# Two pairs of idle transpositions in each gated projection of a decoder trunk, and two other moves on TensorE

## The chip, the cores and the metric

One NeuronCore of a Trainium2 chip. The metric is the time of one execution in device microseconds (us); less is better. Several executions of the same program are given with their median.

## What is computed

Two layers. In each, a gated feed-forward block (SwiGLU, half step), a token mixer of 16 heads in three groups, and a second gated block; at the end a norm. The batch is 1, there are T = 256 tokens, D = 1024 channels, and FF = 2816 hidden channels. All data are float32.

```python
def _rmsnorm(x, g):
    x32 = x.astype(jnp.float32)
    y = x32 * lax.rsqrt(jnp.mean(x32 * x32, axis=-1, keepdims=True) + RMS_EPS)
    return (y * g.astype(jnp.float32)).astype(x.dtype)

def _swiglu(x, w_gate, w_up, w_down):
    return (jax.nn.silu(x @ w_gate) * (x @ w_up)) @ w_down
...
    for l in range(DEPTH):
        x = x + 0.5 * _swiglu(_rmsnorm(x, ffn1_norm[l]), ffn1_w_gate[l], ffn1_w_up[l], ffn1_w_down[l])
        h = _rmsnorm(x, mix_norm[l])
...
        x = x + jnp.concatenate([out_a, out_b, out_c], axis=-1) @ w_out[l]
        x = x + 0.5 * _swiglu(_rmsnorm(x, ffn2_norm[l]), ffn2_w_gate[l], ffn2_w_up[l], ffn2_w_down[l])
    return _rmsnorm(x, final_norm)
```

The heads of the mixer add a bias that depends on the distance of query and key alone, out of a table of 32 rows by 16 heads (`rel_bias_table`).

## The kernel before

**Layout and precision.** x lies transposed in SBUF, channels on partitions: `xs` is 8 blocks of 128 channels by 256 tokens. Weights come as float32 in chunks of 128 x 1024, two chunks to a load of 1 MB on SP's DMA queue, into five buffers (`raw`, RAW = 5). `split` (lines 144 to 160) makes of each chunk a rounded part `whi` (ACT, line 157) and the rest `wlo` (DVE, line 158), three chunks ahead of their use. The operands of x are split likewise into `xx[k]`, both parts side by side. A product of 128 channels by 128 outputs is then two matmuls (`mm2`, lines 289 to 292): `whi` against both parts, 512 columns, and `wlo` against the first, 256 columns. This text calls the two a pair.

**Order on TensorE (PE).** Matmuls and transpositions are chained in the order in which the code issues them (`in_order`, line 211), so nothing overtakes on PE. All other engines' instructions and the DMAs are ordered by the framework's scheduler.

**A gated projection** (`ffn`, line 307; four in all, called first, second, third and fourth here) has 22 steps i of two chunks, 16 pairs each: gate and up sums of 128 hidden channels in two PSUM banks (`pgu`). 352 pairs in all. Then 8 x 22 = 176 pairs of the down projection follow (`pdn`). The norm isn't applied to x ahead of the products: its factor is worked out while they run, and multiplies the sums afterwards. For that, `norm.column()` (matmuls `pss` of the squares' sum against ones, then `ms` on DVE and `rcol` on POOL) is issued behind the first pair of step 2, and `rms_row` (two transpositions `prow` and a copy `rrow` on DVE) behind the tenth pair of it. Counted from 0 over the projection, these pairs are tiles 32 and 41. The constant `AT = (0, 9)` counts them within step 2.

**PSUM** has four banks with the tag "mm" and four with "at". The sums of steps 2, 5, 8 ... lie in "at", as do `pss`, `prow`, the bias table's products and most of the mixer's small results. A tile of a tag waits until an earlier one of the tag has been read.

**The bias table.** `load_bias` (line 387) issues four small loads on SP's queue and comes at step 3 of the first projection; `make_bias` (line 399) comes at step 6: two products `pu` of the table against one-hot distances, a copy each to SBUF on DVE, and a chain of DMAs on SP's queue: rows `u` to memory, 128 copies of them (`w`), and back as `bias` in the form that the mixer adds.

**The end.** The last projection's down products give a block k of x every 22 pairs. DVE adds it to x (lines 366 and 295), ACT squares two blocks at a time (line 243), POOL adds the squares up, ACT makes `y` (x by the gain, line 371, tag "A" with three buffers), and PE transposes it into `turned` (`turn`, line 375): block k - 1 behind the down products of block k, so inside the stream. Behind the last block come `pss` on the earlier sum and on both last squares, turn 7, `ms`, `rcol`, the scaling of `turned` and the store.

Of the kernel before, what the change touches and what calls it, by code (L numbers as in the profile page):

```python
# [39 lines left out]
AT = (0, 9)  # L40
# [38 lines left out]
def tile_trunk(ctx, tc, xT, gains, kvg, sinks, table, onehot, wgu, wdn, winv, wins, wkv, wout, out):  # L79
# [146 lines left out]
    class Norm:  # L226
# [11 lines left out]
        def square(self, k, last=False, after=None):  # L238

            if k % 2 == 0:  # L240
                return
            sq = tmp.tile([P, 2, T], F32, tag="sq2", name="sq", bufs=2)
            behind(nc.scalar.activation(sq, xs[:, k - 1:k + 1, :], AF.Square), after)  # L243
            if len(self.sums) == 0 or (last and k == DK - 1):
                self.sums.append(sq)
            else:
                s = tmp.tile([P, 2, T], F32, tag="ss", name="ss", bufs=2)
                nc.gpsimd.tensor_add(s, self.sums[0], sq)  # L248
                self.sums = [s]
            if k == DK - (3 if last else 1):  # L250
                s = tmp.tile([P, T], F32, tag="fold", name="fold", bufs=1)
                nc.gpsimd.tensor_add(s, self.sums[0][:, 0, :], self.sums[0][:, 1, :])
                self.sums = [s]
            elif k == DK - 1:
                self.sums = [self.sums[0], sq[:, 0, :], sq[:, 1, :]]
# [51 lines left out]
    def ffn(norm, nxt, last=False, first=None, between=(), at=AT):  # L307
        hs, banks, ws = [], {}, {}

        def products(i, h, start=0, stop=DK):  # L310

            if start == 0:
                ws[0] = next_w(ahead=(i, h) not in ((1, 1), (2, 0)))
                if h == 0:
                    for m in range(2):
                        banks[i, m] = bank("pgu", "at" if i % 3 == 2 else "mm")
            whi, wlo = ws[0]
            for j in range(start, stop):
                k, m = h * DK // 2 + j // 2, j % 2
                c = slice(j * P, (j + 1) * P)  # L320
                mm2(banks[i, m], whi[:, c], wlo[:, c], xx[k], k == 0, k == DK - 1)


        products(0, 0)
        products(0, 1)
        if first:
            first()
        products(1, 0)
        products(1, 1)
        for n in range(2 * DK):  # L330
            products(2, n // DK, n % DK, n % DK + 1)
            if n == at[0]:
                col = norm.column()
                for m in range(2):
                    split(cursor[0] + SPLIT_AHEAD - 2 + m)
            if n == at[1]:
                row = rms_row(col)
        for i in range(FK):
# [7 lines left out]
            nc.vector.tensor_mul(t, g, row)  # L346
# [3 lines left out]
            nc.gpsimd.tensor_mul(sr, s, row)  # L350
# [5 lines left out]
        for k in range(DK):  # L356
# [7 lines left out]
            if last and k:  # L364
                turn(k - 1)
# [3 lines left out]
            if last:  # L369
                ys[k] = tmp.tile([P, T], F32, tag="A", name="y")  # L370
                nc.scalar.activation(ys[k], x[k], AF.Copy, scale=nxt.g(k))
# [15 lines left out]
    def load_bias():  # L387
        nc.sync.dma_start(out=kvgain, in_=kvg)
# [3 lines left out]
        tab = tmp.tile([NBUCK + 1, NH], F32, tag="tab", name="tab", bufs=1)  # L392
        nc.vector.memset(tab[NBUCK:NBUCK + 1, :], NEG)
        nc.sync.dma_start(out=tab[:NBUCK, :], in_=table)
        oh = act.tile([NBUCK + 1, 2, NDIST], F32, tag="oh", name="onehots")
        nc.sync.dma_start(out=oh, in_=onehot)
        early.extend((tab, oh))
# [331 lines left out]

    for l in range(DEPTH):  # L730
        nxt = Norm(3 * l + 1)
        ffn(norm, nxt, first=first_squares if l == 0 else None, between={3: load_bias, 6: make_bias} if l == 0 else {})
# [95 lines left out]
```

## Time and profile before

| what | us |
|---|---|
| median of three executions | 966.33 |
| these three | 972.0, 965.53, 966.33 |
| the profiled execution | 971.86 |
| its span, from the first instruction to the last | 970.1 |
| PE busy in it | 957.8 |
| DVE, ACT and POOL busy | 689.7, 554.5, 182.5 |

The profile comes from one more execution, whose own time stands in the table; the difference between its time and its span lies around the program. The records of matmuls have modelled ends, so distances between their starts tell more than their durations. A product of two float32 operands (`pu`, `pss`) leaves two records, a transposition one.

### The profile page before, as it was taken

Reading aid. Unit: us, or ns where it says so; the run is one execution under the profiler, and the core shown is the slowest. Engines: PE = TensorE matmul, PEld = TensorE weight load, DVE = VectorE, ACT = ScalarE, POOL = GpSimd, SP = SyncE. Lnnn points to the kernel's source line nnn. Section 1 sums busy time; section 2 is a strip of 40 time slices with the busy share of each in tenths; the row PEclk is TensorE's granted clock in tenths of the full one; section 3 lists DMA queues with packets and bytes.
Section 4 is the critical chain, followed back from the end, with each engine's and each line's share of the span. In section 5 each row is a group of like instructions: output and inputs, shape, how many; then the busy total and the mean of one; then the engine's idle time right before and its main releaser. Section 6 shows DMA issues by size and latency. Waiting matters only on the chain.

```text
span 970.1 us, 15601 instructions
## 1 busy us (share of the span) xinstructions
PE 957.8 (99%) x5924; PEld 846.5 (87%) x5924; DVE 689.7 (71%) x1235; ACT 554.5 (57%) x1024; POOL 182.5 (19%) x156
## 2 busy tenths in 40 slices
PE   8999999999999999999999999999999999999996
PEld 7888888898999888888888888889989988888885
DVE  5787775659747877776668777666795588777552
ACT  6655554446876655554446556544488566555442
POOL 3221110121313212210022211001132042211001
PEclk9999999999999999999999999999999999999998
DMA  8688545553424565555556555555433346555511
GB/s 336 222 301 296 201 174 179 178 188 126 156 93 174 178 212 175 177 198 189 175 179 208 177 190 201 175 181 190 150 130 133 131 174 217 174 180 202 184 44 43
DMA packets 47575, 174.41 MB, mean 180 GB/s; under 512 B 3291, under 2 KB 5867, under 8 KB 47372
## 3 DMA queue, kind: packets, MB, share of 16 engines
q1 hardware_dynamic: 47212, 172.90, 51.3%
q8 instruction: 46, 0.75, 0.3%
q10 hardware_dynamic: 288, 0.52, 0.1%
q14 instruction: 29, 0.24, 0.1%
HBM read 172.34 MB, written 4.22 MB: 182 GB/s over the span
## 4 chain that ended last, share of the span: by engine, by line
PE 90%; issue 3%; DVE 2%; ACT 2%; POOL 1%; DMA 1%; SPq 0%; POOLq 0%; DVEq 0%; ACTq 0%
PE pgu L215 50%; PE pdn L215 22%; PE pp L215 7%; PE pwo L215 5%; PE pv L215 2%; PE po L215 1%; PE pt L218 1%; POOL ss L248 1%; PE psc L215 1%; DVE acc L499 1%; ACT whi L157 1%; DMA raw<-wgu 1%; DVE m L498 1%; ACT e L576 0%; PE pi L215 0%
## 5 line engine op out<-in xcount | busy, mean ns | idle before, releaser
L215 PE MATMUL pgu<-xx,whi 128*128 128x512 f32 x1408 | 498.1, 398 | 1.6 <-ACT whi L157 1.6
L158 DVE TENSOR_TENSOR wlo<-raw,whi 128x1024 fp32r<-128x1024 f32 (+3 forms) x314 | 383.3, 1223 | 141.2 <-ACT whi L157 134.4
L157 ACT CAST whi<-raw 128x1024 fp32r<-128x1024 f32 (+2 forms) x322 | 332.6, 1034 | 250.0 <-PE pdn L215 110.4
L215 PE MATMUL pgu<-xx,wlo 128*128 128x256 f32 x1408 | 396.0, 281 | 0.0
L215 PEld LDWEIGHTS pgu<-xx,whi 128*128 128x128 f32 x1408 | 265.1, 188 | 66.0 <-ACT whi L157 1.9
L215 PEld LDWEIGHTS pgu<-xx,wlo 128*128 128x128 f32 x1408 | 266.8, 189 | 0.3 <-DVE wlo L158 0.3
L215 PE MATMUL pdn<-h,whi 128*128 128x512 f32 x704 | 248.5, 397 | 0.0
L215 PE MATMUL pdn<-h,wlo 128*128 128x256 f32 x704 | 197.6, 281 | 0.0
L350 POOL TENSOR_TENSOR sr<-s,rrow 128x256 f32<-128x256 f32 x88 | 98.0, 1113 | 357.4 <-ACT s L348 357.1
L215 PEld LDWEIGHTS pdn<-h,whi 128*128 128x128 f32 x704 | 132.1, 188 | 31.7
L215 PEld LDWEIGHTS pdn<-h,wlo 128*128 128x128 f32 x704 | 133.0, 189 | 0.0
L302 ACT COPY b<-pgu 128x256 f32<-128x256 f32 x176 | 65.3, 372 | 82.2 <-PE pgu L215 82.2
L304 DVE TENSOR_TENSOR a<-pgu,b 128x256 f32<-128x256 f32 x176 | 73.5, 420 | 26.1 <-ACT b L302 25.5
L215 PE MATMUL pp<-xx,whi 128*128 128x256 f32 x480 | 90.7, 289 | 0.0
L215 PEld LDWEIGHTS pp<-xx,whi 128*128 128x128 f32 x480 | 74.2, 191 | 2.7 <-issue 1.7
L215 PE MATMUL pp<-xx,wlo 128*128 128x256 f32 x240 | 67.7, 282 | 0.0
L352 DVE TENSOR_TENSOR h<-sr,a 128x256 f32<-128x256 f32 x88 | 37.4, 425 | 29.0 <-POOL sr L350 28.7
L215 PE MATMUL pwo<-ohl,whi 128*128 128x256 f32 x256 | 47.7, 287 | 0.0
L248 POOL TENSOR_TENSOR ss<-sq 128x512 f32<-128x512 f32 x7 | 10.2, 1457 | 196.8 <-ACT sq L243 196.8
L215 PEld LDWEIGHTS pp<-xx,wlo 128*128 128x128 f32 x240 | 45.8, 191 | 0.0
L354 ACT CAST h<-h 128x256 fp32r<-128x256 f32 x88 | 35.3, 401 | 18.3 <-DVE h L352 18.3
L348 ACT ACTIVATE s<-t 128x256 f32<-128x256 f32 x88 | 37.4, 425 | 5.8 <-DVE t L346 5.5
(99 smaller groups left out, 718.1 us busy)
## 6 DMA issues: line engine op xcount, KB each, us to landing
raw<-wgu SPq DMA_DIRECT2D x86, 1024.0 KB, 5.0
raw<-wdn SPq DMA_DIRECT2D x44, 1024.0 KB, 5.0
raw<-wins SPq DMA_DIRECT2D x14, 1024.0 KB, 4.9
raw<-wout SPq DMA_DIRECT2D x8, 1024.0 KB, 4.9
raw<-winv SPq DMA_DIRECT2D x4, 776.0 KB, 4.2
w<-u SPq DMA_DIRECT2D x1, 3072.0 KB, 13.9
bias<-w SPq DMA_DIRECT2D x1, 2048.0 KB, 9.9
raw<-wgu SPq DMA_DIRECT2D x3, 512.0 KB, 7.7
```

Source lines behind the costliest of these rows:

```text
L157: ops = (nc.scalar.copy(hi[:, a:b], raw(n, a, b)), low.tensor_sub(lo[:, a:b], raw(n, a, b), f(hi[:, a:b])))
L158: low.tensor_sub(lo[:, a:b], raw(n, a, b), f(hi[:, a:b])))
L215: in_order(nc.tensor.matmul(*a, **kw))
L218: in_order(nc.tensor.transpose(*a))
L248: nc.gpsimd.tensor_add(s, self.sums[0], sq)
L302: nc.scalar.copy(b, p[:, T:])
L304: nc.vector.tensor_add(a, p[:, :T], b)
L348: nc.scalar.activation(s, t, AF.Silu)
L350: nc.gpsimd.tensor_mul(sr, s, row)
L352: nc.vector.tensor_mul(h, sr, u)
L354: nc.scalar.copy(hs[i][:, 0, :], h)
L498: nc.vector.max(out=m8, in_=acc[:, cs])
```

## The change

It does six things.

1. `ffn` counts its pairs through (`tile_no`), and `AT = (32, 41)` names the same two places as before.
2. Behind tiles 44 and 48 of each of the four projections a bank of the tag "at", called `step`, is taken, and two transpositions of the identity are written to it. Nobody reads them.
3. `make_bias` is issued in the first projection behind tile 32, ahead of `norm.column()`, in place of step 6. The loads of the table and the one-hots go to ACT's DMA queue and are issued ahead of the first projection (`load_bias`); the mixer's small scales keep their place at step 3 (`load_scales`).
4. In the last projection, `turn(0)` to `turn(6)` are issued in one run behind the down products of block 7, no longer one by one between them.
5. `y` lies in the buffers of the tags "E" and "ET", four each, instead of "A".
6. For the last norm, the squares of blocks 6 and 7 are taken one by one; POOL adds the square of block 6 to the sum, so `pss` has two operands there, not three.

```diff
-AT = (0, 9)
+
+
+AT = (32, 41)
+STEP = (44, 48)
...
         def square(self, k, last=False, after=None):
 
+            if last and k > DK - 3:
+                sq = tmp.tile([P, T], F32, tag="sq2", name="sq", bufs=2)
+                nc.scalar.activation(sq, x[k], AF.Square)
+                if k == DK - 2:
+                    s = tmp.tile([P, T], F32, tag="ss", name="ss", bufs=2)
+                    nc.gpsimd.tensor_add(s, self.sums[0], sq)
+                    self.sums = [s]
+                else:
+                    self.sums.append(sq)
+                return
             if k % 2 == 0:
                 return
...
-            if len(self.sums) == 0 or (last and k == DK - 1):
+            if len(self.sums) == 0:
...
-            elif k == DK - 1:
-                self.sums = [self.sums[0], sq[:, 0, :], sq[:, 1, :]]
...
-    def ffn(norm, nxt, last=False, first=None, between=(), at=AT):
+    def ffn(norm, nxt, last=False, first=None, ahead=None, between=()):
...
+        tile_no = [0]
+        col, row = [], []
+
+        def products(i, h):
+
+            whi, wlo = next_w(ahead=(i, h) not in ((1, 1), (2, 0)))
+            if h == 0:
+                for m in range(2):
+                    banks[i, m] = bank("pgu", "at" if i % 3 == 2 else "mm")
+            for j in range(DK):
                 k, m = h * DK // 2 + j // 2, j % 2
                 c = slice(j * P, (j + 1) * P)
                 mm2(banks[i, m], whi[:, c], wlo[:, c], xx[k], k == 0, k == DK - 1)
...
+                if tile_no[0] == AT[0]:
+                    if ahead:
+                        ahead()
+                    col.append(norm.column())
+                    for m in range(2):
+                        split(cursor[0] + SPLIT_AHEAD - 2 + m)
+                if tile_no[0] == AT[1]:
+                    row.append(rms_row(col[0]))
+                if tile_no[0] in STEP:
+                    p = bank("step", "at")
+                    for b in range(2):
+                        transpose(p[:, b * P:(b + 1) * P], ident, ident)
+                tile_no[0] += 1
+
+
+        for i in range(3):
+            for h in range(2):
+                products(i, h)
+            if i == 0 and first:
+                first()
...
-            if last and k:
-                turn(k - 1)
+            if last and k == DK - 1:
+                for i in range(k):
+                    turn(i)
...
             if last:
-                ys[k] = tmp.tile([P, T], F32, tag="A", name="y")
+                ys[k] = tmp.tile([P, T], F32, tag=("E", "ET")[k % 2], name="y", bufs=4)
                 nc.scalar.activation(ys[k], x[k], AF.Copy, scale=nxt.g(k))
...
     def load_bias():
+        tab = tmp.tile([NBUCK + 1, NH], F32, tag="tab", name="tab", bufs=1)
+        nc.vector.memset(tab[NBUCK:NBUCK + 1, :], NEG)
+        nc.scalar.dma_start(out=tab[:NBUCK, :], in_=table)
+        oh = act.tile([NBUCK + 1, 2, NDIST], F32, tag="oh", name="onehots")
+        nc.scalar.dma_start(out=oh, in_=onehot)
+        early.extend((tab, oh))
+
+    def load_scales():
         nc.sync.dma_start(out=kvgain, in_=kvg)
...
+    load_bias()
     for l in range(DEPTH):
         nxt = Norm(3 * l + 1)
-        ffn(norm, nxt, first=first_squares if l == 0 else None, between={3: load_bias, 6: make_bias} if l == 0 else {})
+        if l == 0:
+            ffn(norm, nxt, first=first_squares, ahead=make_bias, between={3: load_scales})
+        else:
+            ffn(norm, nxt)
```

On PE, behind the first pair of step 2 of the first projection, stood before (whi and wlo are the weight's parts, xx the operand of x, fold the sum of the squares):

```order
L215 MATMUL pgu<-xx_103,whi_184 128x512 [waits Activation_49]
L215 MATMUL pgu<-xx_103,wlo_185 128x256 [waits DVE_49]
L215 MATMUL pss<-ones,fold 128x1 [waits Pool_49]
L215 MATMUL pss<-ones,fold 128x1
L215 MATMUL pgu<-xx_103,whi_184 128x512
```

and stands now:

```order
L218 MATMUL pgu<-xx_103,whi_189 128x512 [waits Activation_49]
L218 MATMUL pgu<-xx_103,wlo_190 128x256 [waits DVE_49]
L218 MATMUL pu<-onehots,tab 8x384 [waits DMAHW2_49,DMAHW0_49]
L218 MATMUL pu<-onehots,tab 8x384
L218 MATMUL pss<-ones,fold 128x1 [waits PE_49,Pool_49]
L218 MATMUL pss<-ones,fold 128x1
L218 MATMUL pgu<-xx_103,whi_189 128x512 [waits DVE_49]
```

The two products of the bias table have come in ahead of pss, and the pair behind pss waits for DVE, which gives a bank back.

On PE, at the tenth pair of step 2 of the second projection, stood before (rcol is the norm's factor by token):

```order
L218 MATMUL prow<-ident,rcol 128x128 [waits Pool_49]
L218 MATMUL prow<-ident,rcol 128x128
L215 MATMUL pgu<-xx_108,whi_3509 128x512
L215 MATMUL pgu<-xx_108,wlo_3510 128x256
L215 MATMUL pgu<-xx_108,whi_3509 128x512
L215 MATMUL pgu<-xx_108,wlo_3510 128x256
L215 MATMUL pgu<-xx_109,whi_3509 128x512
L215 MATMUL pgu<-xx_109,wlo_3510 128x256
L215 MATMUL pgu<-xx_109,whi_3509 128x512
```

and stands now:

```order
L221 MATMUL prow<-ident,rcol 128x128 [waits Pool_49]
L221 MATMUL prow<-ident,rcol 128x128
L218 MATMUL pgu<-xx_108,whi_3515 128x512
L218 MATMUL pgu<-xx_108,wlo_3516 128x256
L218 MATMUL pgu<-xx_108,whi_3515 128x512
L218 MATMUL pgu<-xx_108,wlo_3516 128x256
L218 MATMUL pgu<-xx_109,whi_3515 128x512
L218 MATMUL pgu<-xx_109,wlo_3516 128x256
L221 MATMUL step<-ident 128x128 [waits DVE_49]
L221 MATMUL step<-ident 128x128
L218 MATMUL pgu<-xx_109,whi_3515 128x512
```

Three pairs behind prow the first step has come in; the second stands four pairs further.

On PE, at the program's end, stood before (pdn are the down products, y the blocks to be turned):

```order
L215 MATMUL pdn<-h_10041,wlo_10474 128x256
L218 MATMUL turned<-ident,y 128x128 [waits Activation_49]
L218 MATMUL turned<-ident,y 128x128
L215 MATMUL pss<-ones,fold 128x1 [waits Pool_49]
L215 MATMUL pss<-ones,fold 128x1
L215 MATMUL pss<-ones,sq 128x1 [waits Activation_49]
L215 MATMUL pss<-ones,sq 128x1 x3
L218 MATMUL turned<-ident,y 128x128 [waits Activation_49]
L218 MATMUL turned<-ident,y 128x128
```

and stands now:

```order
L218 MATMUL pdn<-h_10065,wlo_10484 128x256
L221 MATMUL turned<-ident,y 128x128 [waits PE_49]
L221 MATMUL turned<-ident,y 128x128 x7
L221 MATMUL turned<-ident,y 128x128 [waits PE_49]
L221 MATMUL turned<-ident,y 128x128 x3
L221 MATMUL turned<-ident,y 128x128 [waits Activation_49]
L221 MATMUL turned<-ident,y 128x128
L218 MATMUL pss<-ones,ss 128x1 [waits Pool_49]
L218 MATMUL pss<-ones,ss 128x1
L218 MATMUL pss<-ones,sq 128x1 [waits Activation_49]
L218 MATMUL pss<-ones,sq 128x1
L221 MATMUL turned<-ident,y 128x128 [waits Activation_49]
```

Fourteen transpositions stand in a row behind the last product, and pss has four products in place of six.

## Rows read from the trace of the kernel before

**Rows 1.** The page's first part: busy us, share of the span, instructions.

```profile
PE 957.8 (99%) x5924; PEld 846.5 (87%) x5924; DVE 689.7 (71%) x1235; ACT 554.5 (57%) x1024; POOL 182.5 (19%) x156
```

**Rows 2.** The chain of waits in order of time: start us, us, what.

```profile
26.53 18.73 PE pgu L215 x108
...
46.64 90.65 PE pgu L215 x512
137.29 62.19 PE pdn L215 x352
...
315.58 109.54 PE pgu L215 x620
425.12 62.19 PE pdn L215 x352
487.31 11.66 PE pgu L215 x66
...
502.81 107.48 PE pgu L215 x620
610.30 61.01 PE pdn L215 x352
...
787.32 109.54 PE pgu L215 x620
```

**Rows 3.** Windows by stage: us, engines' busy time (records), granted clock, DMA share, GB/s.

```profile
425.00:487.00 62.00, 62.00 (x353) 53.74 (x352) 38.97 (x48) 28.61 (x36) 3.88 (x3) 1.00 0.55 186
...
610.00:671.00 61.00, 61.00 (x353) 53.80 (x352) 38.38 (x49) 28.14 (x36) 3.90 (x3) 1.00 0.53 184
```

**Rows 4.** Timeline of PE about the first two turned: start us, us, instruction.

```profile
911.88 0.40 PE L215 MATMUL pdn<-h,whi 128*128 128x512 f32 x1
...
912.25 0.38 PE L218 MATMUL turned<-ident,y 128*128 128x128 f32 x2
...
920.24 0.38 PE L218 MATMUL turned<-ident,y 128*128 128x128 f32 x2
```

**Rows 5.** Timeline of PE about prow of the third projection.

```profile
502.07 0.40 PE L215 MATMUL pgu<-xx,whi 128*128 128x512 f32 x1
...
502.43 0.38 PE L218 MATMUL prow<-ident,rcol 128*128 128x128 f32 x2
```

**Rows 6.** Timeline of PE about prow of the second projection.

```profile
314.85 0.40 PE L215 MATMUL pgu<-xx,whi 128*128 128x512 f32 x1
...
315.20 0.38 PE L218 MATMUL prow<-ident,rcol 128*128 128x128 f32 x2
...
316.13 0.40 PE L215 MATMUL pgu<-xx,whi 128*128 128x512 f32 x1
...
316.49 0.40 PE L215 MATMUL pgu<-xx,whi 128*128 128x512 f32 x1
```

**Rows 7.** Timeline of PE about pss and about pu in the first projection.

```profile
22.48 0.61 PE L215 MATMUL pss<-ones,fold 128*128 128x1 f32 x4 [0.76 <-POOL fold L252]
...
45.19 1.45 PE L215 MATMUL pu<-onehots,tab 33*8 33x384 f32 x4
...
46.57 0.50 PE L215 MATMUL pgu<-xx,whi 128*128 128x512 f32 x1
```

**Rows 8.** DMA issues by line: KB each, median us to landing.

```profile
w<-u SPq DMA_DIRECT2D x1, 3072.0 KB, 13.9
...
onehots<-onehot SPq DMA_DIRECT2D x1, 99.0 KB
```

**Rows 9.** Timeline of the end, all engines.

```profile
960.21 0.38 PE L218 MATMUL turned<-ident,y 128*128 128x128 f32 x2
...
961.32 0.63 ACT L243 ACTIVATE sq<-xs 128x512 f32<-128x512 f32 x1 [7.48 <-DVE xs L295]
...
962.00 1.05 PE L215 MATMUL pss<-ones,sq 128*128 128x1 f32 x8 [1.08 <-ACT sq L243]
```

**Rows 10.** Groups of instructions by line and form: ACT's square of 256 elements elsewhere.

```profile
L511 ACT ACTIVATE sq<-pr 128x256 f32<-128x256 f32 x2 | 0.8, 420 | 0.0
```

More of the change, by code (lines that the diff above doesn't have):

```diff
@@ L305, in add_halves @@
         return a
-    def ffn(norm, nxt, last=False, first=None, between=(), at=AT):
+    def ffn(norm, nxt, last=False, first=None, ahead=None, between=()):
         hs, banks, ws = [], {}, {}
[L310 to L318, printed above, removed]
+        tile_no = [0]
[6 more added lines that the diff above has]
+            for j in range(DK):
                 k, m = h * DK // 2 + j // 2, j % 2
@@ L321, in products @@
                 mm2(banks[i, m], whi[:, c], wlo[:, c], xx[k], k == 0, k == DK - 1)
[L324 to L337, printed above, removed]
+                if tile_no[0] == AT[0]:
[16 more added lines that the diff above has]
+                first()
         for i in range(FK):
@@ L345, in ffn @@
             t = tmp.tile([P, T], F32, tag="A", name="t")
-            nc.vector.tensor_mul(t, g, row)
+            nc.vector.tensor_mul(t, g, row[0])
             s = tmp.tile([P, T], F32, tag="B", name="s")
@@ L349, in ffn @@
             sr = tmp.tile([P, T], F32, tag="B", name="sr")
-            nc.gpsimd.tensor_mul(sr, s, row)
+            nc.gpsimd.tensor_mul(sr, s, row[0])
             h = tmp.tile([P, T], F32, tag="h", name="h", bufs=2)
@@ L391, in load_bias @@
         nc.vector.tensor_scalar_mul(nsink, sink, -1.0)
[L392 to L397, printed above, removed]
     def make_bias():
```

## The prediction

> **What bounds the kernel now.** I read the page's first part, then the windows by stage, then the chain of waits in order of time, and last the timeline of PE at the few places where something other than a weight product stands in its queue. The first part says that PE is busy 957.8 us of a span of 970.1 [rows 1]: 12.3 us are left, and nearly all of them lie before the first product and behind the last. In between, waits for DVE, ACT or a DMA take next to nothing from PE, so a change can only take work from PE, add work to it, move work into the two ends, or alter how fast PE works its queue off.
>
> The last is the surprise of this profile. In the chain, the down products of the second gated projection are 352 matmuls in 62.19 us, those of the third the same 352 in 61.01; the 620 gate and up products that stand behind prow take 109.54 us in the second and fourth and 107.48 in the third [rows 2]. Two matmuls (512 columns with whi, 256 with wlo) make a pair: 62.19 / 176 = 0.3534 us, 61.01 / 176 = 0.3466. I call them the slow and the quick pace; they lie 0.0067 us apart. Neither clock nor DMA explains it: both stretches have a granted clock of 1.00 (the 2.4 GHz level) and a DMA share of 0.55 and 0.53 [rows 3]. The pace is carried on: the third projection begins slow (66 matmuls in 11.66 us, 0.3533 a pair) since the second ended slow, and it stays quick through 310 and then 176 pairs once it is quick [rows 2]. It alters only where a small thing stands between pairs. The first projection is quick (108 matmuls in 18.73 us, 0.3469 a pair) until the bias table's products, pu, and slow behind them (512 in 90.65 us, 0.3541) [rows 2]. The third turns quick at its prow.
>
> **The change part by part.** Sums are made against the profiled execution, 971.86 us; the median of the runs shown is 966.33, one of them 972.0. The profiled one lies 5.5 us above the median. The second and fourth projection in quick pace would be worth 6.7 us (below), so my reading is that those two were quick in the median run and slow in the profiled one.
>
> Steps: four projections, two steps of two transpositions each, eight pairs of transpositions. What such a pair adds is read from turned, which has the same form: from 912.25 to 920.24 are 7.99 us [rows 4] for 22 pairs of products at 0.3534 (7.775), so 0.216. Eight add 1.73 us, all on the path, as PE has no gap there. The wait that a step adds is for DVE to give back a bank: the first for the reading of pss, 12 pairs earlier, the second for the copy of prow, 7 pairs or 2.5 us earlier. If that cover failed, PE and everything queued behind it would stand for what is left of the DVE instruction in front of the copy.
>
> What the steps may give back is the pace. Of four prow, one stood in quick pace and left it quick (first projection [rows 2]), one turned slow into quick (third), two stayed slow (second, fourth). In slow pace every third pair is longer, 0.36 against 0.35: the prow that turned it stood behind a long one (502.07 to 502.43) [rows 5], the one of the second projection behind a short one (314.85 to 315.20) [rows 6]. There the third pair behind prow is again long (316.13 to 316.49) [rows 6], and that is tile 44, behind which the first step comes. Against it: the first turned also stood behind a long pair (911.88 to 912.25), and the pace stayed slow, since the next turned came 7.99 us later [rows 4]. So the evidence is divided; I take it that the two steps together bring the second and fourth to quick and leave the first and third so, at somewhat under one half. By pairs: first projection, 256 + 176 = 432 pairs behind the old place of pu, 2.89 us; second, 352 - 45 + 176 = 483 and the 33 that open the third, 516 pairs, 3.46 us; fourth, 483, 3.24 us. Together 9.59 us less. The bounds are 0 and this, and below 0 if the third loses its pace (a rival).
>
> The Trainium skill, "TensorE: Matmul & The Clock Gate", section "Back-to-back issue gap", gives one distance for a number of columns: columns by clock and about 2.5 ns. By that rule a transposition costs its own time and nothing outlasts it, the 9.59 us would not come, and the time would be 971.5 us. The trace disagrees, with 62.19 and 61.01 us for the same 352 matmuls at one granted clock [rows 2, 3].
>
> pu: at its old place it holds PE from 45.19 to 46.57, 1.38 us [rows 7]; that goes. At its new place it stands ahead of pss, where PE idles 0.76 us for the fold on POOL [rows 7]; so 1.38 - 0.76 = 0.62 is added, net 0.76 less. Behind it the second bank of tile 33 waits for DVE's copy of pu, queued behind a wlo split and an add: bounds 0 and 1, I take 0, as pss stands in between. The two loads for it go from SP's to ACT's queue ahead of ACT's first work; 99 KB at the 221 GB/s of the 3,072 KB copy in 13.9 us [rows 8] are 0.45 us at most taken from the first loads, I take 0.2. The writing and rereading of the bias follow on SP some 20 us earlier than before. SP stands 13.9 us for the copy [rows 8], with the weight loads queued behind; each chunk is 8 pairs, 2.8 us, and ten are held, 28 us, which covers it as it did before.
>
> The turns: six of the seven pairs of transpositions inside the stream go, 6 x 0.216 = 1.30 us. In the end, before, turn 6 began at 960.21; DVE added x, ACT began the last square at 961.32, and at 962.00 PE began eight matmul records of pss on it [rows 9], which at 0.11 apiece end at 962.9. Now 14 transpositions of 0.108 fill 960.21 to 961.7, four records of the earlier sum go to 962.2; the square has 256 elements (0.42 [rows 10] for 0.63) and is done before that, and its four records end at 962.6: 0.29 less. If the y's came late, it would be up to 0.5 more.
>
> Sum: + 1.73 - 9.59 - 0.76 + 0.2 - 1.30 - 0.29 = -10.01, so 971.86 - 10.0 = 961.9 us. Against the median that is 0.46% less. A measurement of this kernel can tell about 1%, 9.7 us.
>
> **The rivals.**
> A: the steps leave the slow pace where it is, in the second and fourth. For it speaks the first turned [rows 4], against it the third projection's prow [rows 5]. 961.9 + 3.46 + 3.24 = 968.6 us.
> B: no pace alters against the profile; moving pu does not help the first projection either, as pss and prow behind it leave it slow. 961.9 + 9.59 = 971.5 us. The Trainium skill's rule named above gives this case.
> C, slower than before: the steps take the quick pace away, in the third projection too, as pu did in the first [rows 2]. From its step on, 483 pairs more are slow, 3.24 us: 974.7 us, above the median by 8.4 and above the profiled execution by 2.9. It decides if a step stands where it throws quick into slow; against it, the first prow left quick as it was.
> D: SP's stand for the bias holds up weight loads so near the start that the store of ten chunks isn't full; if none of the 13.9 us is hidden, 975.8 us. Against it: the same stand before left no wait on PE.
> E: the 5.5 us between the median and the profiled execution are not pace but something the profiled one alone has; then all of the sum comes off the median, 966.33 - 10.0 = 956.3 us.
>
> **How the numbers follow.** The forecast 0.48; A 0.22; B 0.10; C 0.07; D 0.03; E 0.10. Predicted is 961.9. The range of 957.5 to 971.5 takes in the forecast with A and B and their small terms, and leaves out C, D and E, 0.20 together. Faster by over 1% (under 956.7) is E, 0.10; slower by over 1% (over 976.0) is D and the upper end of C, 0.04; within 1% is the rest, 0.86.
>
> **What would show it right or wrong.** In the chain after: 352 down products in about 61.0 us in all four projections, or 62.2 where a step failed; the gate and up products quick or slow from tile 49 on; the eight steps as two transpositions each of 0.22 us with no wait ahead; no wait on fold before the first pss; pu gone from 45 us; 14 turns in a row behind the last product, and pss's last record 0.3 us nearer to it. Wrong would be any wait of PE on a DMA or whi between 25 and 60 us, a step that waits for DVE, or a pace that changes where nothing stands between pairs.

## The result, and the profile after

| | before | after |
|---|---|---|
| median, us | 966.02 (9 executions, 963.26 to 972.0) | 975.04 (9 executions, 974.41 to 975.73) |
| ratio, 95% interval | | 1.0096 [1.0075, 1.0116] |
| profiled execution, us | 971.86 | 974.71 |
| its span, us | 970.1 | 972.9 |

The changed kernel is slower by 0.96%, 9.0 us between the medians and 2.9 between the profiled executions. Before, executions of one program lie up to 9 us apart; after, 1.3 us. That difference in spread turns out to be the key to the result.

The page's first part of the kernel after (busy us, share of the span, instructions), which answers to [rows 1]:

```profile
PE 962.2 (99%) x5936; PEld 847.8 (87%) x5936; DVE 692.5 (71%) x1235; ACT 554.4 (57%) x1025; POOL 182.6 (19%) x157
```

PE has 4.4 us more busy time for 12 more records; 10.7 us of the span are left without it, as against 12.3. The kernel isn't waiting more. PE takes longer for nearly the same work, so the view to read is the chain of waits, of the kernel after (start us, us, what), against [rows 2]:

```profile
21.71 1.38 PE pu L218 x4
23.09 0.54 PE pss L218 x4
...
30.10 107.05 PE pgu L218 x606
137.15 62.19 PE pdn L218 x352
...
316.43 0.22 PE step L221 x2
316.64 1.42 PE pgu L218 x8
318.06 0.22 PE step L221 x2
318.28 107.06 PE pgu L218 x606
425.34 62.18 PE pdn L218 x352
...
504.02 0.22 PE step L221 x2
504.24 1.39 PE pgu L218 x8
...
505.85 107.06 PE pgu L218 x606
612.91 62.19 PE pdn L218 x352
...
794.05 107.06 PE pgu L218 x606
901.11 54.42 PE pdn L218 x308
```

Divide before comparing: 606 matmuls are 303 pairs, and 107.06 / 303 = 0.3533 us a pair in each of the four projections; the down products take 62.19 / 176 = 0.3534, in the fourth 54.42 / 154 = 0.3534. Every projection is at the slow pace behind its second step. The third is the one to look at. Before, it was quick from prow on (107.48 and 61.01 us [rows 2]). Now the 8 matmuls between its two steps still take 1.39 us, 0.347 a pair; in the second projection the same 8 take 1.42, 0.355 a pair, and in the fourth too. So the first step left these two as slow as it found them. Behind the second step the third projection is as slow as the others, and it stays so for 303 and 176 pairs.

Clock and DMA again say nothing about it. The windows of the second and third projection's down products of the kernel after (us, busy time of PE, PEld, DVE, ACT, POOL, granted clock, DMA share, GB/s), against [rows 3]:

```profile
425.00:487.00 62.00, 62.00 (x352) 53.77 (x352) 39.02 (x49) 28.75 (x36) 3.88 (x3) 1.00 0.55 187
613.00:675.00 62.00, 62.00 (x353) 53.81 (x352) 38.27 (x48) 27.75 (x36) 3.87 (x3) 1.00 0.53 180
```

Both have the granted clock of 1.00, the 2.4 GHz level, as both had before. The DMA share in the third projection is 0.53 at 62.19 us, and it was 0.53 at 61.01.

### The profile page after: what moved, and what is told of

Same layout as the page of the kernel before. It is cut to its first block, busy times and chain, and to the rows that moved or that the text cites. A ratio compares the mean times of both kernels' runs of the same rounds, so it can differ in the third digit from the quotient of the medians.

```text
span 972.9 us, 15617 instructions
## 1 busy us (share of the span) xinstructions
PE 962.2 (99%) x5936; PEld 847.8 (87%) x5936; DVE 692.5 (71%) x1235; ACT 554.4 (57%) x1025; POOL 182.6 (19%) x157
## 4 chain that ended last, share of the span: by engine, by line
PE 94%; DVE 2%; ACT 1%; issue 1%; DMA 1%; SPq 0%; POOLq 0%; POOL 0%; DVEq 0%; ACTq 0%
PE pgu L218 51%; PE pdn L218 25%; PE pp L218 7%; PE pwo L218 5%; PE pv L218 2%; PE po L218 1%; PE pt L221 1%; PE psc L218 1%; DVE acc L518 1%; DMA raw<-wgu 1%; DVE m L517 1%; ACT e L595 0%; PE pi L218 0%; PE pss L218 0%; ACT e L613 0%
```

## The experiments

All kernels are timed beside the kernel before on the same chip. Diffs are against the changed kernel where the text does not name the kernel before.

### Which part of the change is it

First the change without its steps, and the kernel before with the steps alone.

```diff
-STEP = (44, 48)
+STEP = ()
```

> The change without its steps. Theory P (a step throws a quick pace into the slow one, and the slow one stays to the projection's end): the changed kernel's first and third projection were quick behind prow and between the two steps, so without steps both stay quick for 486 pairs at 0.0067 us less, 3.25 us each, and 8 x 0.216 = 1.73 us of steps go: 975.0 - 1.7 - 6.5 = 966.8 us, and 352 down products in 61.0 us in the first and third, 62.2 in the second and fourth. Should the second and fourth also be quick in some executions, those lie 6.7 us lower still, at 960. Theory F (a step costs its own time and nothing outlasts it; something else in the change slows the pace): 975.0 - 1.7 = 973.3 us, and 62.2 us of down products in all four.

Measured: 965.61 us (963.0 to 966.77, 10 executions), ratio 0.9995 [0.9979, 1.0011].

```diff
+STEP = (44, 48)
...
+        def step(n):
+            if n in STEP:
+                p = bank("step", "at")
+                for b in range(2):
+                    transpose(p[:, b * P:(b + 1) * P], ident, ident)
...
+            step(32 + n)
...
-            if i > 2:
+            if i == 3:
+                products(i, 0, 0, 1)
+                step(48)
+                products(i, 0, 1)
+                products(i, 1)
+            elif i > 2:
```

> The kernel before with the steps alone: bias products at their old place, turns inside the stream, squares as before. Theory P: all four projections slow behind the second step, so against the profiled execution of before (971.9, in which the third was quick behind prow and the first until the bias products) + 1.7 of steps + 3.3 of the third + 0.3 of the first: 977 us, 62.2 us for each 352 down products. Theory F: the median of before 966.0 + 1.7 = 967.7 us, with the third still at 61.0.

Measured: 976.6 us (976.23 to 976.72, 4 executions), ratio 1.0122 [1.0105, 1.014].

The loss goes with the steps and comes with the steps. In the chain of waits of the run without steps, the third projection is quick behind prow, and the fourth has the same 107.48 us:

```profile
501.91 107.48 PE pgu L218 x620
609.40 61.01 PE pdn L218 x352
```

and in that of the run with the steps alone, the third is slow behind the second step, as after the change. There it is slow from the first step on (1.41 us for the 8 matmuls between the steps, with a pair of 0.36 among them):

```profile
504.92 1.41 PE pgu L216 x8
506.55 107.06 PE pgu L216 x606
613.61 62.18 PE pdn L216 x352
```

These two runs also give what the other edits are worth. With steps in both, all projections are slow in both, and 976.72 - 974.71 = 2.0 us lie between the profiled executions (1.6 between the medians); the forecast had 0.76 - 0.2 + 1.30 + 0.29 = 2.15. This checks their sum, not each of them.

### One step alone

```diff
-STEP = (44, 48)
+STEP = (44,)
```

> The change with only the first step of each projection, behind tile 44. Theory P1 (it is the second step, four pairs behind the first, that throws quick into slow; the first left the first and third quick): 975.0 - 0.9 - 2 x 3.2 = 967.7 us, down products of the first and third at 61.0 us. Theory P2 (any step in quick pace ends it within a few pairs): 975.0 - 0.9 = 974.1 us, all four at 62.2. Theory F: 974.1 too, but with the pace slow before the step as well.

Measured: 967.58 us (964.32 to 970.89, 10 executions), ratio 1.0037 [1.0022, 1.0053]. Its profiled execution took 964.32 us; three of its projections are quick, the second is slow.

```diff
-STEP = (44, 48)
+STEP = (48,)
```

> The change with only the second step, behind tile 48. Theory P1a (a step leaves quick quick if it comes out of an undisturbed quick stretch; the second failed because it followed the first by four pairs): 967.7 us, first and third at 61.0 us for 352 down products. Theory P1b (the place behind tile 48 itself throws it, for what stands there besides): 974.1 us, all four at 62.2, with the first and third quick up to tile 48.

Measured: 970.28 us (966.73 to 970.79, 8 executions), ratio 1.0047 [1.0031, 1.0063]. Its profiled execution took 970.79 us, with the second projection alone quick. The third shows that no second step is needed to lose the pace. It is quick between prow and its only step (2.45 / 7 = 0.350, which has the longer first pair behind prow in it), and slow behind the step:

```profile
499.47 2.45 PE pgu L218 x14
501.92 0.22 PE step L221 x2
502.14 107.06 PE pgu L218 x606
```

At the same place in the second projection the same step, also in a quick pace (2.44 us for 14), left it quick: 105.04 us for 606.

One step, then, doesn't fix the pace: some projections come out quick, others slow, and executions spread over 4 to 7 us. The tight 975 comes with the pair of steps. From the chain of the run with the first step alone, the third projection:

```profile
500.55 0.22 PE step L221 x2
500.77 106.43 PE pgu L218 x614
607.20 61.01 PE pdn L218 x352
```

106.43 / 307 = 0.3467: the first step leaves it quick.

### Is it the second step, or its being only four pairs behind the first

```diff
-STEP = (44, 48)
+STEP = (44, 90)
```

> The changed kernel with its second step moved from tile 48 to tile 90. Shift theory (in quick pace one pair of transpositions is borne, a second one throws the pace to slow, however far apart they are): behind tile 44 a projection is quick, as with the first step alone, and behind tile 90 it is slow to its end; the 42 pairs between are worth 0.28 us a projection, so about 974 us and every down product at 0.3534 us a pair. Spacing theory (it is the distance of four pairs that throws it): the second step finds a settled quick pace and leaves it, so the time is that of the first step alone, 967.6, and 0.9 for the four further pairs of transpositions, 968.5 us.

Measured: 973.99 us (973.86 to 974.77, 4 executions), ratio 1.0094 [1.007, 1.0118]. The third projection in its chain of waits:

```profile
503.73 0.22 PE step L221 x2
503.95 15.95 PE pgu L218 x92
520.12 92.22 PE pgu L218 x522
612.35 62.19 PE pdn L218 x352
```

The 92 matmuls between the steps are quick (15.95 / 46 = 0.3467); behind tile 90 the pace is slow (92.22 / 261 = 0.3533) to the end of the projection. The second and fourth show the same 15.95 and 92.22. The pace was settled for 46 pairs, with nothing between them, and changed at the second step, so the spacing of four alone isn't what does it. One rival is left: 4 and 46 are both one more than a multiple of three, the length of the slow pace's cycle (below). Only one projection that was quick had another remainder, 17 pairs in the run with three steps below, and it lost the pace too. The gain between the steps, 46 x 0.0067 = 0.31 us in each of three projections, is most of the 1.05 us by which this run lies under the changed kernel.

Half the disturbance at each place:

```diff
-                    for b in range(2):
+                    for b in range(1):
```

> The changed kernel with one transposition in each step in place of two, at the same tiles 44 and 48. Work taken away: 8 x 0.108 = 0.86 us. If any second break in the row of pairs throws the pace to slow, all four projections end slow and the time is 975.0 - 0.9 = 974.2 us. If what counts is how long the break is (two transpositions, 0.216 us), two halves do what one whole step does: three of four projections quick, about 967.5 us.

Measured: 966.81 us (960.99 to 974.25, 10 executions), ratio 1.0009 [0.9985, 1.0034]. Two single transpositions don't throw every projection slow, as two pairs of them do. They don't leave all of them alone either: in the profiled execution, 967.42 us, the first and fourth are quick, the second and third slow (the second was so ahead of them), and one execution took 974.25. So halving a step changes what comes behind it, and "any break in the row of pairs" is too simple.

### Could prow's place do what the steps were meant to do

In the trace before, the pair that stands ahead of prow seemed to decide [rows 5, 6]. Four runs moved prow by one pair and kept pss behind tile 32.

```diff
-AT = (32, 41)
-STEP = (44, 48)
+AT = (32, 40)
+STEP = ()
```

> The change without steps, and prow one pair earlier (AT = 32, 40). In slow pace every third pair is long (0.361 us; the others 0.349 and 0.350). In the profiles so far every prow behind the pair next after a long one left the pace slow, and every prow behind the long one or the one ahead of it made it quick. In the first and fourth kind of opening (long pairs at tiles 34, 37, 40) tile 41 is the bad place and tile 40 a good one; in the other (long at 35, 38, 41) tile 40 is good too. Theory P (the place of prow in the cycle of three decides): all four projections quick behind prow, 61.0 us for 352 down products, and against the profiled execution without steps (966.4, third and fourth quick) 6.5 us less: 959.9. Theory R (which pace comes out is chance from execution to execution): 963 to 967 as without the move, with one or two of four quick.

Measured: 966.88 us (966.28 to 970.43, 12 executions), ratio 1.0016 [0.9997, 1.0035]: a miss for the rule as I then had it.

```diff
-AT = (32, 41)
-STEP = (44, 48)
+AT = (32, 42)
+STEP = ()
```

> The change without steps, and prow one pair later (AT = 32, 42). Theory P: with long pairs at tiles 34, 37, 40 the place behind tile 42 lies ahead of a long one and is good: quick; with long pairs at 35, 38, 41 it is the bad one: slow. So the projections that were slow behind tile 41 turn quick and those that were quick turn slow: 963 to 967 us, each projection's pace as its opening says. Theory R: paces unrelated to the opening.

Measured: 966.05 us (962.98 to 969.75, 10 executions), ratio 0.9991 [0.9971, 1.0012]. This doesn't tell the two theories apart: the median fits both, and two of the executions, 969.45 and 969.75, lie above the range of the first.

The kernel before with prow one pair earlier:

```diff
-AT = (0, 9)
+AT = (0, 8)
```

> The kernel before with one number changed: prow one pair earlier, AT = (0, 8). Theory P: second, third and fourth projection quick in every execution, the first until the bias products at 45 us as before: 971.9 - 3.4 - 3.2 = 965.2 us against the profiled execution of before, and no execution above 966. Theory R: 963.3 to 972 as before.

Measured: 968.34 us (963.43 to 972.59, 12 executions), ratio 1.0031 [1.0008, 1.0053]: a miss too, though its profiled execution, 963.43 us, is quick behind prow in the last three projections. There the fourth turns slow again at the first turned, among the down products (88 of them in 15.25 us ahead of it, 0.3466 a pair, 44 in 7.78 behind, 0.3536).

And the change with its steps, prow one pair earlier:

```diff
-AT = (32, 41)
+AT = (32, 40)
```

> The whole change, with prow one pair earlier, so that prow leaves the pace quick (if the theory of the place holds). Theory P2 (the second step ends the quick pace wherever it came from): 975 us again, all four at 62.2 us for 352 down products. Theory P3 (the steps only keep what prow leaves): all four quick, 959.9 + 1.7 = 961.6 us.

Measured: 975.46 us (975.3 to 975.6, 4 executions), ratio 1.0095 [1.0068, 1.0123]. In its profiled execution all four projections are quick behind prow. Behind the first step the last three still are (1.39 us for 8 matmuls; the first projection has 1.41, and a pair of 0.36 ahead of its second step), and behind the second all four are slow. Whatever prow's place had brought didn't outlast the steps.

Why moving prow alone was no use shows in the openings of the projections: the pace between pss and prow isn't the same from one run to the next. At tile 32 pss can come before POOL's fold is ready ([rows 7]: 0.76 us of waiting in the first projection; in the kernel after pss takes 0.45 us in the second projection and 0.34 in the third, which I took for a wait of 0.1 in the second). So the next runs moved both places, pss by three pairs.

```diff
-AT = (32, 41)
-STEP = (44, 48)
+AT = (35, 43)
+STEP = ()
```

> The changed kernel without steps, with pss behind tile 35 in place of 32 and prow behind tile 43 in place of 41. Three pairs later the fold on POOL is ready and pss does not wait. If that wait, of another length in each execution, is what makes the opening pace and so the time differ between executions, the executions now agree within about 1 us, at a level between 960 (all four projections quick behind prow) and 973.3 us (all slow). If the spread comes from elsewhere, executions lie over 963 to 970 us with a median near 966, as without steps at the old places.

Measured: 969.96 us (969.83 to 973.16, 6 executions), ratio 1.0061 [1.0039, 1.0083].

```diff
-AT = (32, 41)
-STEP = (44, 48)
+AT = (35, 44)
+STEP = ()
```

> As the run with pss behind tile 35 and prow behind tile 43, with prow one pair later, behind tile 44. If the opening is the same in each execution, prow now stands at the next place of the cycle of three pairs, and the projections' paces behind it differ from those of that run in a fixed way, with executions again within about 1 us of each other. If the opening differs between executions, 963 to 970 us as there, and no fixed difference between the two kernels.

Measured: 960.76 us (959.88 to 963.61, 10 executions), ratio 0.996 [0.9942, 0.9978]. **This is the fastest kernel of the study**, 0.4% under the kernel before and 14 us under the changed one. The second projection in the chain of the run with prow behind tile 43:

```profile
308.76 0.34 PE pss L218 x4
309.10 2.94 PE pgu L218 x16
312.03 0.22 PE prow L221 x2
312.25 108.83 PE pgu L218 x616
421.07 62.19 PE pdn L218 x352
```

and with prow behind tile 44:

```profile
308.66 0.34 PE pss L218 x4
309.00 3.28 PE pgu L218 x18
312.29 0.22 PE prow L221 x2
312.50 106.44 PE pgu L218 x614
418.95 61.01 PE pdn L218 x352
```

pss now takes 0.34 us in this projection of both. The two kernels have the same instructions on PE, one pair further on at prow, and are 9.2 us apart: 108.83 / 308 = 0.3533 against 106.44 / 307 = 0.3467 from there to the projection's end. The expected difference came, but not the expected 1 us between executions of one kernel: each has two levels about 3.1 us apart (969.9 and 973.0; 960.3 and 963.4), as if one projection still varied.

One pair further:

```diff
-AT = (32, 41)
-STEP = (44, 48)
+AT = (35, 45)
+STEP = ()
```

> The changed kernel without steps, pss behind tile 35, prow behind tile 45: one pair later than in the run at 960.76 us, two later than in the run at 969.96. Cycle theory: prow now stands behind the third pair of the cycle in the second and fourth projection, which so far turned quick in five places of six: 960 to 964 us. If quick and slow alternate from place to place: about 970 us, as with prow behind tile 43.

Measured: 963.81 us (962.92 to 967.26, 10 executions), ratio 0.9989 [0.997, 1.0008]; in the profiled execution, 963.1 us, all but the third are quick. The median lies in the range of the cycle theory, though four of the ten executions took 966.4 to 967.3. Then the kernel before with the new places alone:

```diff
-AT = (0, 9)
+AT = (3, 12)
```

> The kernel before with its two places three pairs later: pss behind tile 35, prow behind tile 44, nothing else altered. If the place alone gives what the run at 960.76 us has, the second to fourth projection are quick behind prow; the first, where pu follows at step 6, is slow or not. Other edits of the change are worth 2.3 us, so 963 us with a quick first projection and 966 with a slow one. If the place gains only together with pu moved to the front, the time is that of before, 966 with executions from 963 to 970.

Measured: 964.62 us (961.99 to 964.92, 10 executions), ratio 0.9976 [0.9958, 0.9994]. The places alone give part of the gain; the first projection is slow from pu on, as before. The fourth is quick behind prow, stays quick behind the first turned among its down products (44 matmuls in 7.63 us) and is slow behind the second (43 in 7.67): one pair of transpositions borne, the next one not, as with the steps.

### The steps again, at a good place of prow, and a third step

```diff
-AT = (32, 41)
-STEP = (44, 48)
+AT = (35, 44)
+STEP = (47, 51)
```

> The run with pss behind tile 35 and prow behind tile 44 (960.76 us, quick behind prow in all four projections in its profiled execution), with the two steps of the change put back three and seven tiles behind prow, as in the change (tiles 47 and 51). Theory that the second step throws the quick pace away: all down products at 0.3534 us a pair, 960.8 + 1.7 + 4 x about 3.1 = about 975 us. Theory that the change only had the bad luck of its prow's place: 960.8 + 1.7 = 962.5 us.

Measured: 975.08 us (974.78 to 975.8, 4 executions), ratio 1.0085 [1.0056, 1.0114]. The fourth projection in its chain:

```profile
793.37 0.22 PE step L221 x2
793.59 1.39 PE pgu L218 x8
794.98 0.22 PE step L221 x2
795.20 106.00 PE pgu L218 x600
901.20 54.42 PE pdn L218 x308
```

Quick between the steps (1.39 us for 8), slow behind the second (106.00 / 300 = 0.3533). Against the fastest kernel, whose instructions are the same but for the steps, that is 14.3 us, of which the steps' own time is 1.7. The place of prow isn't what made the change slow.

```diff
-STEP = (44, 48)
+STEP = (44, 48, 65)
```

> The changed kernel with a third step, behind tile 65, where the slow cycle of three pairs has been settled for 16 pairs. Cycle theory (what a pair of transpositions does to the slow pace depends on which pair of the cycle it stands behind: behind the first it stays slow, behind the two others it turns quick): in the profiled execution, if it opens as the changed kernel did, the second to fourth projection turn quick behind tile 65, the first doesn't; 975.0 + 0.9 for four more pairs of transpositions - 3 x 3.1 = about 966.6 us. Number theory (two or more pairs of transpositions behind prow always end slow): all down products at 0.3534 us a pair and 975.9 us.

Measured: 975.8 us (972.57 to 975.97, 4 executions), ratio 1.0083 [1.005, 1.0116]. A third step doesn't bring the pace back: the last three projections were slow ahead of it and stayed slow. One thing doesn't fit "the second step always throws it": the first projection was slow between its first two steps (1.41 us for 8 matmuls, with a pair of 0.36 among them), quick behind the second, and turned slow at the third.

```profile
30.34 0.22 PE step L221 x2
30.56 5.90 PE pgu L218 x34
...
36.68 101.05 PE pgu L218 x572
```

5.90 / 17 = 0.347 between the second and the third step, 101.05 / 286 = 0.3533 behind. And one of the four executions, not a profiled one, took 972.57 us, 3.1 us under the next, as if one projection had stayed quick to its end.

### What the runs say together

Six kernels are the changed one without steps, with pss and prow at different places. They do the same work, and their profiled executions sort by the number of projections that are quick to their end:

| pss, prow behind tiles | quick projections | profiled execution, us |
|---|---|---|
| 35, 43 | 1 | 969.88 |
| 32, 40 | 1 | 970.13 |
| 32, 41 | 2 | 966.36 |
| 32, 42 | 3 | 963.03 |
| 35, 45 | 3 | 963.1 |
| 35, 44 | 4 | 959.88 |

From each number of quick projections to the next it is 3.1 to 3.8 us, and a quick projection was put at 3.24 to 3.46. With its steps' time taken off, the changed kernel fits in as a line with none: 974.71 - 1.7 = 973.0. In the profiled executions of the six kernels with two or three whole steps, 24 projections of 24 are slow behind the last one; in the six above, 14 of 24 are quick.

What makes prow turn the pace is described, not explained. The slow pace is a cycle of three pairs (0.349, 0.350 and 0.361 us from whi to whi, 1.060 together; a quick pair takes 0.3467). In the nine profiled executions without steps, prow stood behind the first of the cycle 7 times and the pace stayed slow each time; behind the second 6 times and it turned quick each time; behind the long one 11 times and it turned quick 10 times. Where prow found the pace quick or mixed (by turns 0.350 and 0.344, the same 0.347 on the mean), it was quick behind it 7 times of 12, and these sort by the pair ahead as well: in the quick pace 4 times of 4, behind a short pair of the mixed one 3 of 3, behind a long one 0 of 5. So in 35 of the 36 cases the pair ahead of prow tells the pace behind it; the exception is a prow that came 0.75 us after the pair ahead of it had begun. That is sorted after the fact; the runs that moved prow were set on a part of it. But the third step stood behind the second of the cycle three times, and the pace stayed slow, against the expectation. So the rule holds for prow as far as seen and not for a step, and what lies under the two paces stays open.

A whole step sorts in another way. Behind a long pair of the slow pace, where prow turned it quick 10 times of 11, a step left it slow 11 times of 11. And of 29 steps in the second to fourth projections that came in a quick pace, 14 began 0.345 to 0.347 us after the last whi and left the pace quick, 15 began 0.348 to 0.350 us after it and lost it. All 11 second steps among them are of the latter kind; so are the lone step that lost the pace above (0.348, against 0.345 for the one that kept it) and three first steps. So being the second may not be what counts. What sets these 2 or 3 ns wasn't tested, nor whether they are a cause or a sign.

## Why the prediction was wrong

The forecast was 961.9 us, and 974.71 was measured in the profiled execution. By its own steps:

- **The step that failed** is "I take it that the two steps together bring the second and fourth to quick and leave the first and third so". They leave all four slow. The forecast rested it on a step that stands behind a long pair, as prow did in the third projection. The first step did stand behind a long pair (0.36 us) in the second and fourth, as forecast, and the pace stayed slow (1.42 us for 8 matmuls, 0.355 a pair); the second step brought nothing either, and the third projection lost its pace at it. The term of -9.59 us came out at +3.24 for the third projection, 0 for the second and fourth, and some +0.4 for the first, whose gate and up products are slow from 23 us on, but for a few pairs, instead of from pu at 45 (63 pairs at 0.0067). The 2.89 us hoped for in the first didn't hang on the steps alone: in the run without steps it was slow too (109.53 and 62.18 us). With 3.24 in place of -9.59 the forecast's sum is 971.86 + 1.73 + 3.24 - 0.76 + 0.2 - 1.30 - 0.29 = 974.7, the time measured; that it fits to the tenth is luck, since small errors of some tenths cancel (below).
- What the traces had shown was that one small thing between pairs can turn the pace either way. The forecast took from two places that looked alike [rows 5, 6] that a step behind a long pair turns slow into quick, and let the two steps count as one chance each. It didn't ask what the second step does to a pace that the first has left quick. Where the first does leave it quick, as in the run with steps behind tiles 44 and 90, it was slow behind the second, in every profiled execution with whole steps.
- Rival C gave 974.7 us by the mechanism that came, "the steps take the quick pace away, in the third projection too", at 0.07. The reason held against it, that prow left the first projection quick, is true of one pair of transpositions in a quick pace and says nothing of the next ones.
- The median as the measure: the forecast read the 5.5 us between the median and the profiled execution as two quick projections. That holds in kind: executions of the kernel before lie from 963 to 972 us, and the table shows some 3.4 us for each projection. Since the profiled execution was one of the slowest, 2.9 us against it are 9.0 against the median. The time of rival E, 956.3, didn't come; that the 5.5 us are two projections is inferred from the table, as no execution near that median was profiled for the kernel before.
- The steps' own cost was right: each is 0.22 us in the chain, and none waits. The 2.0 us (1.6 by medians) measured for the other edits together come near the forecast's 2.15.
- pu: gone from 45 us, it now stands at 21.71 and hides the wait for the fold, as worked out. PE's instructions of the kernel after from 20 to 60 us, grouped (names, forms, count, busy us, mean ns, idle before):

```profile
L218 PE MATMUL pu<-onehots,tab 33*8 33x384 f32 x4 | 1.5, 483 | 0.0
L221 PE MATMUL step<-ident 128*128 128x128 f32 x4 | 0.8, 272 | 0.0
L218 PE MATMUL pss<-ones,fold 128*128 128x1 f32 x4 | 0.6, 255 | 0.0
```

  The last column is 0.0 in these and in the groups of pgu and prow, which are left out: no wait for the fold, for a bank of DVE's, or for a weight chunk while SP copies the bias rows (13.0 us, [rows 8]: 13.9). Rival D is out. The 0.2 us at the start can't be told from chance: in runs with the same instructions up to there, pu begins at 21.42, 21.62, 21.71 and 22.15.
- The end: the timeline behind the last product, of the kernel after,

```profile
963.13 1.69 PE L221 MATMUL turned<-ident,y 128*128 128x128 f32 x14
...
964.30 0.42 ACT L245 ACTIVATE sq<-xs 128x256 f32<-128x256 f32 x1 [7.00 <-DVE xs L306]
...
965.02 0.58 PE L218 MATMUL pss<-ones,sq 128*128 128x1 f32 x4
...
965.47 0.41 PE L221 MATMUL turned<-ident,y 128*128 128x128 f32 x2
```

  and the last turned of the kernel before, which [rows 9] don't have:

```profile
962.92 0.41 PE L218 MATMUL turned<-ident,y 128*128 128x128 f32 x2
```

  From the first turned behind the products to the last it is now 2.34 us, before 962.92 - 960.21 = 2.71: 0.37 less, forecast 0.29. But most of it is lost again behind the store's issue: from the last record of turned to the end of the span it is 7.3 us, before 7.0, and in all profiled executions 7.0 with the old end and 7.3 to 7.6 with the new one. So about 0.1 us is left of the term of 0.29, and what makes the store longer wasn't tested. The 14 transpositions run in a row with no wait for y, and pss on the last square waits for nothing, as the smaller square is done at 964.72.
- One thing about the turns was missed: in a fourth projection that is quick, the first or second turned among the down products throws it slow (the kernel before with prow behind tile 40, and with the places 35 and 44). Setting them in one run is worth up to 132 x 0.0067 = 0.9 us more there (the pairs behind the first turned), beside the 1.30 of their own time.

The rule of the Trainium skill, "TensorE: Matmul & The Clock Gate", section "Back-to-back issue gap", one distance for a number of columns (the section calls its formula that of an isolated matmul), would have made the time 971.5 us. It doesn't hold here: the same 352 matmuls take 61.01 or 62.19 us at one granted clock, in the kernel before, in the runs without steps and with one, and the pace changes at a pair of transpositions and holds for the 480 pairs behind it.

## What to carry to other kernels

Where a tensor engine that is 99% busy works through long rows of equal matmuls, divide the chain's pieces by their counts, stage by stage: two paces 2% apart may stand in one profile, and several executions with levels at even distances are a sign that stages switch between them. Small instructions between the pairs can switch the pace for hundreds of pairs, so the place of one that is needed anyway is worth a scan over a few neighbouring places (969.96, 960.76 and 963.81 us for three of them here), with several executions of each. Don't add instructions to set the pace unless a run shows what the last of them leaves behind, and don't carry over what another instruction of the same form did: prow turned the pace behind a long pair, and a step of the same two transpositions didn't.

## What the runs showed of the hardware

- A pair of 512 and 256 columns is issued at 0.3467 or at 0.3533 us, at a granted clock of 1.00 and the same DMA share. Each pace is kept for as long as the row of pairs isn't broken, over 479 pairs in the third projection of the kernel after, and in the long rows of the gated projections no run showed it change for good but where something stood between pairs.
- Moving two transpositions by one pair, with the same instructions otherwise, changed the median by 9.2 us of 970.
- Two or three steps of two transpositions left 24 projections of 24 slow behind the last step in the profiled executions; two steps of one transposition left two of four quick; a lone step left four of eight quick. Whether the count of transpositions, their time, how the step meets the pairs ahead of it or something else is what counts wasn't settled.
- Equal executions of one program differ by whole projections, 963 to 972 us in the kernel before, and whether pss's wait for the fold is part of that isn't shown. With pss and prow three pairs later, where pss doesn't wait in the later projections, executions of the kernel before lie 2.9 us apart, but those of the change without steps 3.7, as much as the 3.8 at the old places, on two levels 3.1 us apart.
